# Differential attention: the first two weight units of the output projection are prepared piece by piece between the heads

## The chip, the cores and the metric

The kernel runs as one program on one core of a Trainium2 chip. The core has a matmul engine (PE, with its weight loads shown apart as PEld), a vector engine (DVE), a scalar engine (ACT), a general engine (POOL) and a queue engine (SP) that issues most of the transfers. Each engine works through its own instructions strictly in the order in which they were queued, and semaphores tie the engines together. The metric is the device time of one execution in microseconds; the time of a kernel is the median of several runs.

## The reference

One inference step of a two-layer decoder. Layer 0 is gated linear attention, layer 1 differential attention; a squared-ReLU MLP and a layer norm follow each. There are 1024 new prompt tokens behind 16 meta tokens, and eight running sequences with a paged cache of 4096 keys. The change touches layer 1's prompt attention and the projection behind it. Cut to what matters:

```python
q, k, v = diff_project(x, w_in, pos)                 # 8 heads, each with two 64-wide q/k halves
s = einsum('bqhmd,bkhmd->bhmqk', q, k) * 64 ** -0.5  # two score maps per head
p = softmax(where(k_pos <= q_pos, s, -inf))
o = einsum('bhqk,bkhe->bqhe', p[:, :, 0] - lam * p[:, :, 1], v)
out = (rms_norm(o, g_sub) * (1 - lam_init)) @ w_out  # w_out is 1024 x 1024
x = layer_norm(ALPHA * x + out)
```

## The kernel before

All matrix products are taken in a split form: an fp32 operand is cast to a shorter type (`hi`) and the rest (`lo` = operand - `hi`) is kept beside it, and three matmuls make one product. A weight matrix is therefore handled in *units* of 1024 rows by 256 columns. `unit` (L182 to L196) makes one from four *pieces*. A piece is a transfer of 256 KB into a tile `raw` (L191, issued by SP), a cast into `whi` on ACT (L193) and a subtraction into `wlo` on POOL (L194). The pool of `raw` has two buffers, those of `whi` and `wlo` have two each, so two units can be held, and the transfer of a piece must wait until the subtraction two pieces earlier is done. `kunit` (L198) calls `unit` on a slice of columns.

Prompt attention is a list of 64 steps: 8 heads times 8 tiles of 128 query rows. In heads 0 to 6 the tiles come in the order 7, 1, 5, 3, 6, 0, 4, 2, counted by n = 0 to 7; tile t looks at 16 + 128(t+1) keys. A step has two halves:

- `front` (L1348): the two score maps on PE in blocks of up to 512 keys (L1366), masking and row minimum on DVE (L1368), two exponentials with row sums on ACT (L1370), the reciprocal and the combination of the two maps on DVE (L1372 to L1374). The last of these, L1374, is appended to `joined`; its width tells the tile (1040 is n = 0, 656 is n = 6).
- `back` (L1378): transposes of the combined map on PE (L1387), in groups of up to four key blocks, each copied to SBUF by ACT (L1389, appended to `copied`), and the product with the values on PE (L1392). Tile 7 has groups of 512, 512 and 128 columns; tile 6 has 512 and 512; tile 5 has 512 and 384.

Every fourth step ACT moves the result out (L1493) and takes four sums of squares (L1497). Score maps have five buffers (`scp`). Between the steps lie the preparation of the next head's keys and queries (`prep`, with a cast on ACT and a subtraction on DVE, L202 and L203), the loads of the next heads by SP (`load_qk` L1224, `load_v` L1337), the scaling of finished heads on DVE (`scale_piece`, L1410, in pieces of 128x512, two at the end of heads 2, 4 and 6 and two at the start of heads 3 and 5; its power is taken on POOL, L1403) and, at the end of head 3 and in head 4, the projection of the eight samples (`samples_rows`, weight rows `sw` loaded at L1439 by SP, products at L1449 on PE).

The text of the program is not the order on an engine. A planner walks through it with a cost model, gives each instruction a priority by its place in the text, and appends it to its engine's queue when the model says that it is ready and nothing of higher priority is. `tc.issue_after(ins)` adds one tie: instructions written in its block that run on the engine of `ins` are queued behind `ins`. Transfers, which SP issues, and subtractions on POOL get no such tie when `ins` is on ACT.

`w_out` (L1045) multiplies by the output weights, in the order of (unit, half of the tokens) (0,0), (1,0), (0,1), (1,1), (2,0), (3,0), (2,1), (3,1), and takes a unit in when its number comes up first. It is written behind the attention, and its first products run beside head 7. For unit 0 it uses the tie (L1051):

```python
with tc.issue_after(out_after) if scaled and u == 0 else nullcontext():
    units[u] = kunit(w, u * 256)
```

where `out_after` is the latest transposed copy that the text has reached at head 2, n = 3 (L1480), which is the last copy of tile 5 of that head.

Of the kernel before, what the change touches and what calls it, by code (L numbers as in the profile page):

```python
# [11 lines left out]
F32 = mybir.dt.float32  # L12
F32R = mybir.dt.float32r
# [3 lines left out]
ALU = mybir.AluOpType  # L17
# [4 lines left out]
P = 128  # L22
# [92 lines left out]
def hybrid_step(ctx, tc, A, dbg=None, upto=9):  # L115
    nc = tc.nc
    V, S, G, TE = nc.vector, nc.scalar, nc.gpsimd, nc.tensor
    dma = nc.sync.dma_start
# [5 lines left out]
    wsp = ctx.enter_context(tc.tile_pool(name="wsp", bufs=2))  # L124
    wrp = ctx.enter_context(tc.tile_pool(name="wrp", bufs=2))
# [56 lines left out]
    def unit(n, *srcs):  # L182

        hi = wsp.tile([P, 2048], F32R, name="whi")
        lo = wsp.tile([P, 2048], F32R, name="wlo")
        at = 0
        for src in srcs:
            step = 512 // n
            for x in range(0, src.shape[1], step):
                raw = wrp.tile([P, 512], F32, name="raw")  # L190
                dma(raw.rearrange("p (k n) -> p k n", n=n), src[:, x : x + step, :])  # L191
                c = slice(at, at + 512)
                S.copy(hi[:, c], raw)  # L193
                G.tensor_tensor(lo[:, c], raw, hi[:, c].bitcast(F32), op=ALU.subtract)  # L194
                at += 512
        return hi, lo  # L196

    def kunit(w, c0):  # L198
        return unit(256, w.rearrange("(k p) n -> p k n", p=P)[:, :, c0 : c0 + 256])
# [322 lines left out]
    first = proj(0)  # L522
# [10 lines left out]
    for k in range(NB):  # L533
        w = sload(wi[k * P : (k + 1) * P, 0:2048])
# [6 lines left out]
    for k in range(0, NB, 2):  # L541
        w = sload2(wi[:, 2048:3072], k)
# [56 lines left out]
    for hh in range(2):  # L599
        ps = smt()  # L600
        for i in range(2):
            h = 2 * hh + i
# [16 lines left out]
    for s in (8, 4, 2, 1):  # L619
        u = t2()[:, :128]  # L620
# [231 lines left out]
    for h in range(GH):  # L852
        hi, lo = kunit(wi, 2048 + h * 256)
# [188 lines left out]

    def w_out(w, scaled, side=None):  # L1045

        units = {}
        n = 0
        for u, c in ((0, 0), (1, 0), (0, 1), (1, 1), (2, 0), (3, 0), (2, 1), (3, 1)):
            if u not in units:  # L1050
                with tc.issue_after(out_after) if scaled and u == 0 else nullcontext():  # L1051
                    units[u] = kunit(w, u * 256)
            hv, lv = (x.rearrange("p (k n) -> p k n", n=256) for x in units[u])
            for i2 in range(2):
                ps = mmt()
                t0 = 4 * c + 2 * i2
                for i in range(2):
                    a = slice((t0 + i) * P, (t0 + i + 1) * P)
                    for k in range(NB):
                        mm3(ps[:, i * 256 : (i + 1) * 256], XH[:, k, a], XL[:, k, a], hv[:, k, :], lv[:, k, :], k == 0, k == NB - 1)  # L1060
                yv = Yt[:, t0 : t0 + 2, u * 256 : (u + 1) * 256]
                pv = ps.rearrange("p (i n) -> p i n", n=256)
                if scaled:
                    steps_v.append(V.tensor_tensor(yv, yv, pv, op=ALU.add).ins)
                else:
                    steps_v.append(V.scalar_tensor_tensor(yv, yv, ALPHA, pv, ALU.mult, ALU.add).ins)
                if side and (n == 4 if scaled else n < 12):
                    next(side)
                n += 1
                if u % 2:  # L1070
                    for t in (t0, t0 + 1):
                        yield t, u // 2
# [9 lines left out]
    def normalize(steps, stats, done, last=None, behind=None):  # L1082

        st, mv, rs = stats
        half = set()
        for t, j in steps:
            if last and t not in (2, 3):
                if t in half:
                    last(t, mv, rs)
                half.add(t)  # L1090
                continue
            V.bn_stats(st[:, t, j, :], Yt[:, t, j * 512 : (j + 1) * 512])  # L1092
            if t not in half:
                half.add(t)
                continue
            V.bn_aggr(mv[:, t, :], st[:, t])  # L1096
            if t % 2 == 0 and not last:
                continue
            ts = slice(t if last else t - 1, t + 1)
            V.tensor_scalar(rs[:, 0, ts], mv[:, ts, 1], EPS, None, ALU.add)  # L1100
            steps_g.append(G.tensor_tensor(rs[:, 0, ts], rs[:, 0, ts], mhalf[:, : ts.stop - ts.start], op=ALU.pow).ins)
            if last:
                last(t, mv, rs)
                continue
            if behind is not None and t % 4 == 1:
                held = ts
                continue
            for ts in (held, ts) if behind is not None else (ts,):
                with tc.issue_after(behind[-1]) if behind is not None else nullcontext():
                    V.scalar_tensor_tensor(rs[:, 1, ts], mv[:, ts, 0], -1.0, rs[:, 0, ts], ALU.mult, ALU.mult)  # L1110
                for x in range(ts.start, ts.stop):
                    S.activation(Yt[:, x, :], Yt[:, x, :], AF.Identity, bias=rs[:, 1, x : x + 1], scale=rs[:, 0, x : x + 1])
            if t % 4 == 3:
                done(t // 4)

    def to_fm(c, ln, dst=None):
        cs = slice(512 * c, 512 * c + 512)
        for k in range(NB):
            ps = axt()
            for i in range(4):  # L1120
                TE.transpose(ps[:, i * P : (i + 1) * P], Yt[:, 4 * c + i, k * P : (k + 1) * P], ident)
            out = ps if dst is None else dst(c)[:, k, :512]
            g, b = lnp[:, ln, 0, k : k + 1], lnp[:, ln, 1, k : k + 1]
            if k % 2:
                i = V.tensor_scalar(out, ps, g, b, ALU.mult, ALU.add).ins
            else:
                S.activation(out, ps, AF.Identity, bias=b, scale=g)
            if dst is None:
                i = split(XH[:, k, cs], XL[:, k, cs], ps).ins
            steps_v.append(i)  # L1130
# [212 lines left out]
        dma(vx, vr[NM:].rearrange("(t p) d -> p t d", p=P))  # L1343
        return vm, vx

    joined, copied, pend = [], [], []

    def front(h, t, ks, qs):  # L1348
        W = NM + P * (t + 1)
# [111 lines left out]
    for step in steps + [None] * 0:  # L1461
        if step:
            h, n, t = step
            if h < 7:
                if n == 0:
                    nxt = prep(h + 1, *raws[h + 1])
                for _ in range(((1, 1, 2, 0) if h else (0, 1, 1, 2))[n] if n < 4 else 0):
                    heads[h + 1] = next(nxt)
                if n == 3:
                    vals[h + 1] = load_v(h + 1)  # L1470
                elif n == 5 and h < 6:
                    raws.append(load_qk(h + 2))
            if h == 3 and n == 7 or h == 4 and n < 4:
                next(srows)
            todo.append((step, front(h, t, *heads[h])))
            if pend and (h == 7 or (8 * h + n - 6) % 16 < 4):
                with tc.issue_after(joined[-1]):
                    scale_piece()
            if (h, n) == (2, 3):
                out_after = copied[-1]  # L1480
            if (h, n) == (0, 0):
                late(3)
                values_tile()
        if step and len(todo) <= 0:
            continue
        (h, n, t), sc_ = todo.pop(0)
        if n % 4 == 0:
            po = smt()
        at = t % 4 if h == 7 else t // 2
        back(t, sc_, po[:, at * P : (at + 1) * P], *vals[h])  # L1490
        if n % 4 == 3:
            ts = (slice(0, 4), slice(4, 8))[n // 4] if h == 7 else slice(t % 2, 8, 2)
            S.copy(Yd[:, ts, h], po.rearrange("p (t e) -> p t e", e=P))  # L1493
            for i in range(4):
                x = po[:, i * P : (i + 1) * P]
                j = ts.start + i * (ts.step or 1)
                S.activation(x, x, AF.Square, accum_out=oss[:, j, h : h + 1])  # L1497
        if n == 3 and h == 7:
            XH.t[0][1] = xh_part(0, 1)
            o_norm(slice(0, 4), slice(7, 8))  # L1500
            while pend:
                scale_piece()
            for j in range(8):
                o_fm(j, 0)
        elif n == 7 and h < 6 and h % 2:
            o_norm(slice(0, 8), slice(h - 1, h + 1))
        elif n == 7 and h == 6:
            o_norm(slice(0, 8), slice(6, 7))
# [60 lines left out]
    def samples():  # L1569

        sev = s2()
        dma(sev, A["srow"])
        s_post(sev, 2, hp)
        yield

    stats = ln_stats(hp)
    normalize(w_out(A["diff_w_out"][0], True, samples()), stats, lambda c: to_fm(c, 2, xr), None, steps_v)
    if upto == 4:
        dbg(locals())
        return e.close()  # L1580
# [276 lines left out]
```

## Time and profile before

| | |
|---|---|
| time, median of 3 runs | 2794.14 us (2793.73 to 2798.08) |
| the profiled execution's own time | 2787.8 us |
| its span, first to last instruction | 2785.6 us |
| mean granted clock of PE | 0.996 |
| busy share PE / DVE / ACT / POOL | 98% / 69% / 41% / 39% |
| attention heads, 1742 to 2004 us of the span | PE 239.88 of 262 us |
| behind them to the second MLP, 2004 to 2075 us | PE 71.00 of 71 us |

Rows of the view in order of time give the start in us from the span's start, the length in us, engine, line, operation, output<-inputs, shapes, and a count where equal neighbours are merged; in brackets stands the idle time of the engine before the instruction, and what ended it. Rows of the view of windows give the stretch, its length, and for each engine the busy time and the number of instructions, then the granted clock of PE, the busy share of the DMA engines and GB/s.

### The profile page before, as it was taken

Reading aid. Unit: us, or ns where it says so; the run is one execution under the profiler, and the core shown is the slowest. Engines: PE = TensorE matmul, PEld = TensorE weight load, DVE = VectorE, ACT = ScalarE, POOL = GpSimd, SP = SyncE. Lnnn points to the kernel's source line nnn. Section 1 sums busy time; section 2 is a strip of 40 time slices with the busy share of each in tenths; the row PEclk is TensorE's granted clock in tenths of the full one; section 3 lists DMA queues with packets and bytes.
Section 4 is the critical chain, followed back from the end, with each engine's and each line's share of the span. In section 5 each row is a group of like instructions: output and inputs, shape, how many; then the busy total and the mean of one; then the engine's idle time right before and its main releaser. Section 6 shows DMA issues by size and latency. Waiting matters only on the chain. (4 is left out here: it accounts for less than half of the span.)

```text
span 2785.6 us, 52274 instructions
## 1 busy us (share of the span) xinstructions
PE 2716.1 (98%) x19849; PEld 2230.6 (80%) x19849; DVE 1908.2 (69%) x3000; ACT 1130.0 (41%) x2316; POOL 1089.4 (39%) x736
## 2 busy tenths in 40 slices
PE   8999999999999999999999999999999999999998
PEld 5867767987777777777799988776899889798986
DVE  5365453678877777777667740787747888978687
ACT  4344463152221221221242112677625646355554
POOL 2112212234344343334323321120025767786775
PEclk9999999999999999999999999999999999999999
DMA  7575645735898898988748995122143554664585
GB/s 237 167 244 192 222 155 185 263 96 186 292 329 317 310 351 297 345 306 314 264 146 319 353 374 182 54 77 80 39 126 73 122 140 103 136 138 106 131 188 119
DMA packets 276392, 562.81 MB, mean 202 GB/s; under 512 B 23510, under 2 KB 144412, under 8 KB 272044
## 3 DMA queue, kind: packets, MB, share of 16 engines
q1 hardware_dynamic: 256076, 522.75, 54.1%
q0 software_dynamic: 20064, 36.71, 8.1%
q8 instruction: 156, 2.56, 0.4%
q14 instruction: 96, 0.79, 0.1%
HBM read 533.00 MB, written 29.52 MB: 202 GB/s over the span
## 5 line engine op out<-in xcount | busy, mean ns | idle before, releaser
L194 POOL TENSOR_TENSOR wlo<-raw,whi 128x512 fp32r<-128x512 f32 x252 | 366.1, 1467 | 715.0 <-ACT whi L193 571.6
L206 PE MATMUL mmt<-whi,XH 128*128 128x256 f32 (+1 forms) x1744 | 519.1, 300 | 1.1 <-DVE ast L1368 0.9
L207 PE MATMUL mmt<-wlo,XH 128*128 128x256 f32 (+1 forms) x1744 | 516.5, 297 | 0.4 <-POOL wlo L194 0.4
L206 PE MATMUL mmt<-XH,whi 128*128 128x512 f32 (+1 forms) x1216 | 434.5, 359 | 4.0 <-DVE HL L203 1.9
L208 PE MATMUL mmt<-XH,wlo 128*128 128x512 f32 (+1 forms) x1216 | 432.1, 356 | 0.2 <-POOL wlo L1681 0.2
L208 PE MATMUL mmt<-whi,XL 128*128 128x256 f32 x1520 | 427.1, 284 | 0.0
L193 ACT CAST whi<-raw 128x512 fp32r<-128x512 f32 x252 | 150.6, 621 | 567.0 <-PE mmt L208 190.2
L206 PEld LDWEIGHTS mmt<-whi,XH 128*128 128x128 f32 x1744 | 326.9, 188 | 38.9 <-issue 23.5
L953 DVE TENSOR_REDUCE sc<-pg 128x16 f32<-128x1024 f32 x256 | 308.6, 1212 | 71.1 <-POOL pg L952 68.6
L207 PEld LDWEIGHTS mmt<-wlo,XH 128*128 128x128 f32 x1744 | 328.3, 188 | 17.4 <-issue 7.2
L207 PE MATMUL mmt<-XL,whi 128*128 128x512 f32 x768 | 307.3, 401 | 0.0
L952 DVE TENSOR_TENSOR pg<-pg,qb 128x1024 f32<-128x1024 f32 x192 | 262.6, 1375 | 62.2 <-DMA pg<-in_cache_k 55.7
L208 PEld LDWEIGHTS mmt<-whi,XL 128*128 128x128 f32 x1520 | 284.5, 188 | 5.5 <-issue 5.0
L206 PEld LDWEIGHTS mmt<-XH,whi 128*128 128x128 f32 x1216 | 229.0, 189 | 51.0 <-issue 10.8
L952 POOL TENSOR_TENSOR pg<-pg,qb 128x1024 f32<-128x1024 f32 x64 | 166.2, 2599 | 258.9 <-DMA pg<-in_cache_k 157.7
L208 PEld LDWEIGHTS mmt<-XH,wlo 128*128 128x128 f32 x1216 | 229.5, 189 | 34.9 <-issue 2.5
L206 PE MATMUL mmt<-whi,HH 128*128 128x512 f32 x512 | 204.7, 401 | 4.6 <-DVE Y L1186 3.1
L208 PE MATMUL mmt<-whi,HL 128*128 128x512 f32 x512 | 203.9, 398 | 0.0
L207 PE MATMUL mmt<-wlo,HH 128*128 128x512 f32 x512 | 203.4, 397 | 0.0
L1681 POOL TENSOR_TENSOR wlo<-rw,whi 128x512 fp32r<-128x512 f32 x92 | 156.2, 1759 | 87.9 <-ACT whi L1680 87.9
L1681 POOL TENSOR_TENSOR wlo<-RW,whi 128x512 fp32r<-128x512 f32 x96 | 165.6, 1752 | 58.0 <-ACT whi L1680 58.0
L207 PEld LDWEIGHTS mmt<-XL,whi 128*128 128x128 f32 x768 | 145.3, 189 | 38.7 <-issue 7.2
(453 smaller groups left out, 5695.0 us busy)
## 6 DMA issues: line engine op xcount, KB each, us to landing
pg<-in_cache_k SPq DMA_DIRECT2D x256, 512.0 KB
pg<-in_cache_v SPq DMA_DIRECT2D x256, 512.0 KB
raw<-in_mlp_w SPq DMA_DIRECT2D x164, 256.0 KB
swt<-in_mlp_w SPq DMA_DIRECT2D x32, 1024.0 KB
rw<-in_mlp_w SPq DMA_DIRECT2D x116, 256.0 KB
RW<-in_mlp_w POOLq DMA_DIRECT2D x96, 256.0 KB, 5.7
swt<-in_gla_w_in SPq DMA_DIRECT2D x12, 1024.0 KB
swt<-in_diff_w_in SPq DMA_DIRECT2D x12, 1024.0 KB
```

The lines of the kernel that those rows point to most:

```text
L193: S.copy(hi[:, c], raw)
L194: G.tensor_tensor(lo[:, c], raw, hi[:, c].bitcast(F32), op=ALU.subtract)
L206: TE.matmul(ps, ah, bh, start=first, stop=False)
L207: TE.matmul(ps, ah, bl, start=False, stop=False)
L208: return TE.matmul(ps, al, bh, start=False, stop=last)
L952: eng.tensor_tensor(pg, pg, qb, op=ALU.mult)
L953: return V.tensor_reduce(sc[:, n, :], pg.rearrange("p (h d) -> p h d", d=64), op=ALU.add, axis=AX.X).ins
L1681: G.tensor_tensor(lo[:, k, :], t, hi[:, k, :].bitcast(F32), op=ALU.subtract)
```

## The change

A generator `unit_pieces` does the same work as `unit` on the same tiles and returns after each piece. The loop of attention calls it in heads 2 to 5 at n = 1 and n = 5: the four pieces of unit 0 in heads 2 and 3, those of unit 1 in heads 4 and 5. Each cast is tied behind the latest transposed copy that the text has reached at that point, which is the last copy of the step before (tile 7 for n = 1, tile 6 for n = 5). `w_out` gets the finished units as an argument; its own tie goes away, and units 2 and 3 are made in it as before.

```diff
+    def unit_pieces(w, c0):
+        hi = wsp.tile([P, 2048], F32R, name="whi")
+        lo = wsp.tile([P, 2048], F32R, name="wlo")
+        src = w.rearrange("(k p) n -> p k n", p=P)[:, :, c0 : c0 + 256]
+        yield hi, lo
+        for at in range(0, 2048, 512):
+            raw = wrp.tile([P, 512], F32, name="raw")
+            dma(raw.rearrange("p (k n) -> p k n", n=256), src[:, at // 256 : at // 256 + 2, :])
+            c = slice(at, at + 512)
+            S.copy(hi[:, c], raw)
+            G.tensor_tensor(lo[:, c], raw, hi[:, c].bitcast(F32), op=ALU.subtract)
+            yield
...
-    def w_out(w, scaled, side=None):
+    def w_out(w, scaled, side=None, units={}):
-        units = {}
+        units = dict(units)
...
             if u not in units:
-                with tc.issue_after(out_after) if scaled and u == 0 else nullcontext():
-                    units[u] = kunit(w, u * 256)
+                units[u] = kunit(w, u * 256)
...
-            if (h, n) == (2, 3):
-                out_after = copied[-1]
+            if 2 <= h < 6 and n in (1, 5):
+                u = h // 4
+                if u not in first:
+                    pieces = unit_pieces(A["diff_w_out"][0], u * 256)
+                    first[u] = next(pieces)
+                with tc.issue_after(copied[-1]):
+                    next(pieces)
...
-    normalize(w_out(A["diff_w_out"][0], True, samples()), stats, ...)
+    normalize(w_out(A["diff_w_out"][0], True, samples(), first), stats, ...)
```

More of the change, by code (lines that the diff above doesn't have):

```diff
@@ L1344, in load_v @@
         return vm, vx
-    joined, copied, pend = [], [], []
+    joined, copied, pend, first = [], [], [], {}
     def front(h, t, ks, qs):
@@ L1576, in hybrid_step @@
     stats = ln_stats(hp)
-    normalize(w_out(A["diff_w_out"][0], True, samples()), stats, lambda c: to_fm(c, 2, xr), None, steps_v)
+    normalize(w_out(A["diff_w_out"][0], True, samples(), first), stats, lambda c: to_fm(c, 2, xr), None, steps_v)
     if upto == 4:
```

## The prediction

> **What bounds the kernel now.** I read the page first: it says whether one engine sets the time.
>
> ```profile
> span 2785.6 us, 52274 instructions
> ...
> PE 2716.1 (98%) x19849; PEld 2230.6 (80%) x19849; DVE 1908.2 (69%) x3000; ACT 1130.0 (41%) x2316; POOL 1089.4 (39%) x736
> ```
>
> PE is busy 98% of the span, and where it idles is what a change can win. The view of windows, asked for the attention heads and for the stretch behind them, shows where that is.
>
> ```profile
> 1742.00:2004.00 262.00, 239.88 (x1883) 189.88 (x1882) 209.26 (x709) 195.68 (x545) 31.57 (x14) 0.98 0.21 62
> 2004.00:2075.00 71.00, 71.00 (x612) 71.00 (x611) 26.93 (x50) 18.27 (x38) 15.36 (x13) 1.00 0.48 139
> ```
>
> In the heads PE idles 262 - 239.88 = 22.1 us while DVE works 80% and ACT 75% of the time: the three pass work round, and a delay on one can reach PE. Behind them PE has no gap, so a time won in the heads is carried to the end.
>
> Next I measured the heads one by one, by the last DVE operation of a step's front (L1374) in the order of time: width 1040 is a head's n = 0, 656 its n = 6.
>
> ```profile
> 1781.09 1.30 DVE L1374 SCALAR_TENSOR_TENSOR as<-as,ast 128x1040 f32<-128x1040 f32 x1
> 1800.59 0.90 DVE L1374 SCALAR_TENSOR_TENSOR as<-as,ast 128x656 f32<-128x656 f32 x1
> ...
> 1811.78 1.30 DVE L1374 SCALAR_TENSOR_TENSOR as<-as,ast 128x1040 f32<-128x1040 f32 x1
> 1831.13 0.90 DVE L1374 SCALAR_TENSOR_TENSOR as<-as,ast 128x656 f32<-128x656 f32 x1
> ...
> 1844.26 1.30 DVE L1374 SCALAR_TENSOR_TENSOR as<-as,ast 128x1040 f32<-128x1040 f32 x1
> 1867.86 0.90 DVE L1374 SCALAR_TENSOR_TENSOR as<-as,ast 128x656 f32<-128x656 f32 x1
> ...
> 1879.05 1.30 DVE L1374 SCALAR_TENSOR_TENSOR as<-as,ast 128x1040 f32<-128x1040 f32 x1
> ...
> 1918.85 1.30 DVE L1374 SCALAR_TENSOR_TENSOR as<-as,ast 128x1040 f32<-128x1040 f32 x1
> 1936.91 0.90 DVE L1374 SCALAR_TENSOR_TENSOR as<-as,ast 128x656 f32<-128x656 f32 x1
> ```
>
> Head 1 takes 1800.59 - 1781.09 = 19.50 us from n = 0 to n = 6 and 11.19 from there to the next head. Head 2 takes 19.35 and then 13.13; head 3 takes 23.60 and then 11.19; head 5 takes 18.06 for its first part. So the end of head 2 and the start of head 3 are long, and that is where ACT casts the two units:
>
> ```profile
> 1832.24 0.48 ACT L1389 COPY aT<-axt 128x384 f32<-128x384 f32 x1 [0.64 <-PE axt L1387]
> 1832.62 1.15 ACT L193 CAST whi<-raw 128x512 fp32r<-128x512 f32 x2
> ...
> 1843.85 0.62 ACT L193 CAST whi<-raw 128x512 fp32r<-128x512 f32 x1 [0.95 <-DMA raw<-in_diff_w_out]
> ...
> 1849.39 0.62 ACT L193 CAST whi<-raw 128x512 fp32r<-128x512 f32 x1 [1.27 <-DMA raw<-in_diff_w_out]
> ...
> 1851.86 0.62 ACT L193 CAST whi<-raw 128x512 fp32r<-128x512 f32 x1
> 1852.38 0.58 ACT L1493 COPY Y<-smt 128x512 f32<-128x512 f32 x1
> ```
>
> All eight casts lie in 1832.6 to 1852.4, not four: unit 1 follows unit 0 at once. A cast holds ACT for 1852.38 - 1851.86 = 0.52 us, and a cast whose piece has not landed holds back all that is queued behind it. From the waits, over heads 2 and 3:
>
> ```profile
> ACT whi L193 <- DMA raw<-in_diff_w_out: 3.0, 3, 1.3
> ```
>
> (total, times, longest.) PE pays for it in two long gaps and, by the window of head 3, in its clock:
>
> ```profile
> 1845.28 0.49 PE L1392 MATMUL smt<-vm,aT 128*128 128x128 f32 x2 [1.83 <-ACT aT L1389]
> 1856.09 0.34 PE L1366 MATMUL prt<-XH 64*128 64x144 f32 x2 [2.19 <-DVE ast L1368]
> 1844.26:1879.05 34.79, 31.52 (x233) 25.47 (x233) 28.84 (x96) 27.24 (x76) 6.75 (x4) 0.90 0.26 77
> ```
>
> The first gap ends with a copy queued behind the cast of 1843.85, the second with DVE work whose exponentials were queued behind the cast of 1849.39. A clock of 0.90 over 34.79 us is 3.5 us of PE time lost.
>
> **The change part by part.** *Removed: the burst.* The end of head 2 is 13.13 - 11.19 = 1.94 us longer than that of head 1, the start of head 3 23.60 - 19.50 = 4.10 longer than head 1's. Together 6.04 us; with head 5's start as the measure (like head 3's it has two scaling pieces) it is 1.94 + 5.54 = 7.48. Head 5 comes behind head 4, which PE's sample products stretch, so it may start ahead; I take 6.04. The burst's own work, 8 x 0.52 + 3.0 = 7.2 us of ACT, is of this size.
>
> Of this, the clock could be a part apart. *By the Trainium skill ("TensorE: Matmul & The Clock Gate", Part 1) the clock halves only after an idle window of about 3.4 us. The trace has no gap as long as that, and yet the clock falls in the window with the gaps of 1.83 and 2.19. By the rule these gaps would not be the cause, and 3.5 of the 6.04 us would stay.* By the row they are, and I count them as removed.
>
> *Added: eight casts at other places.* Put on the old time axis, the casts land behind the last copies of tiles 7 and 6 of heads 2 to 5. Each piece then has some 15 us and its transfer is long done, so the waits of 3.0 us go; each still holds ACT 0.52. Together between 0 and 8 x 0.52 = 4.16 us. What lies there is seen in heads 5 and 4:
>
> ```profile
> 1928.42 0.26 ACT L1389 COPY aT<-axt 128x128 f32<-128x128 f32 x1
> ...
> 1943.35 0.61 ACT L1389 COPY aT<-axt 128x512 f32<-128x512 f32 x1
> ...
> 1905.02 0.59 ACT L1389 COPY aT<-axt 128x512 f32<-128x512 f32 x1 [3.35 <-PE axt L1387]
> ...
> 1932.55 0.49 PE L1392 MATMUL smt<-vm,aT 128*128 128x128 f32 x2 [0.27 <-ACT aT L1389]
> ...
> 1948.42 0.49 PE L1392 MATMUL smt<-vm,aT 128*128 128x128 f32 x2 [0.53 <-ACT aT L1389]
> ```
>
> Behind the cast of n = 5 (after 1943.35) are queued the sums of squares and the exponentials of the next head's first tiles, then the copy for which PE waits 0.53 us: full price, in heads 2, 3 and 5. Behind that of n = 1 (after 1928.42) PE waits 0.27 for ACT once; I charge one of the three such casts in full. In head 4 ACT itself waits 3.35 us for PE, and two casts hide there. Four of eight: 2.08 us. Without head 4's cover it would be 1.04 more.
>
> *Moved: eight subtractions on POOL.* In the burst one scaling piece and one tiny operation of DVE overlap them:
>
> ```profile
> 1844.55 3.82 POOL L194 TENSOR_TENSOR wlo<-raw,whi 128x512 fp32r<-128x512 f32 x2 [3.41 <-ACT whi L193]
> ...
> 1845.47 1.76 DVE L1410 TENSOR_TENSOR Y<-Y,orr 128x512 f32<-128x512 f32 x1
> 1849.24 0.22 DVE L1373 SCALAR_TENSOR_TENSOR ast<-ast,lamv,ls 128x1 f32<-128x1 f32 x1
> 1849.91 0.68 DVE L1410 TENSOR_TENSOR Y<-Y,orr 128x512 f32<-128x512 f32 x1
> 1852.55 1.28 POOL L194 TENSOR_TENSOR wlo<-raw,whi 128x512 fp32r<-128x512 f32 x1 [0.81 <-ACT whi L193]
> ...
> 1852.89 0.96 DVE L1373 SCALAR_TENSOR_TENSOR ast<-ast,lamv,ls 128x1 f32<-128x1 f32 x1
> ```
>
> They take 1.76 for 0.68 and 0.96 for 0.22: 1.08 + 0.74 = 1.82 us for eight subtractions. Spread, each can meet DVE again: from 0 to 8 x 1.28 = 10.2 us; nearest is the row of the same operation, 1.82, of which half on the path makes 0.9. *The Trainium skill ("SBUF — State Buffer", Who interferes with whom) says that DVE and POOL share a pair of ports under an exclusive lock. These rows agree. By that alone each subtraction could cost its 1.28, which is the slower rival below.*
>
> *Moved: eight transfers on SP.* The first two are issued early in either kernel, the others follow the subtractions.
>
> ```profile
> 1706.39 3.80 SPq L191 DMA_DIRECT2D raw<-in_diff_w_out  x2
> ...
> 1834.62 14.14 SPq L191 DMA_DIRECT2D raw<-in_diff_w_out  x6
> ...
> 1891.23 5.74 SPq L1439 DMA_DIRECT2D sw<-in_diff_w_out  x3
> ```
>
> The third to sixth pass the loads of heads 4 to 6, which are needed a head later. The seventh falls at about 1896, among the rows `sw`: queued ahead of one, it could hold it for as long as the fifth subtraction is late. Bounds: 0, and the 1.28 of a subtraction; I take 0. The ninth and tenth, for unit 2, go out at about 1940 instead of in that row of six and two more, and unit 2 is used behind 2004: nothing.
>
> Sum: -6.04 + 2.08 + 0.9 = -3.06 us. The profiled execution would go from 2787.8 to 2784.7. It lies 6.3 us below the median of the runs; on the median, 2794.14 - 3.06 = 2791.1.
>
> **The rivals.** *B, all pieces hide and the heads run like head 5:* 7.48 us won, 2786.7. For it: ACT waits for PE in each head, five score maps buffer the steps. Against: the 0.53 gap stands already without a cast. Chance 0.26.
>
> *C, the clock falls anyway:* the removed part is 6.04 - 3.5, and the sum 2.54 - 2.98 = -0.4 won, 2794.6. For it: the rule above. Against: the window of head 3 with its two gaps. Chance 0.13.
>
> *D, slower: each subtraction stops DVE in the heads.* Before, most fell into DVE's idle time in the burst, when DVE waited for ACT; spread out, they meet a DVE that is 80% busy. At 8 x 1.28 = 10.2 and 2.08 for the casts the sum is 6.3 us slower, 2800.4. It decides once a subtraction costs more than (6.04 - 2.08) / 8 = 0.50 us. Against: 1.82 / 8 = 0.23 before. Chance 0.14.
>
> *E, the change doesn't do what it says:* the tie holds a cast only from one side, and the planner may queue pieces late and close together. Two neighbours then pay a wait of about 1 us each (0.95 and 1.27 above) again, in two or three places: 2 us of the gain go, 2793. Chance 0.07.
>
> **How the numbers follow.** The forecast (A) has 0.40, with its own range 2788 to 2794 (casts wholly hidden, or 4.16 and 1.82 paid). About 0.2% or 5.6 us is what a measurement here can tell. Faster by more than that: B and the edge of A, 0.31. Slower: D, 0.14. The rest, 0.55, is no change. The range leaves out D and a tip of B: 2785 to 2798.5.
>
> **What would show it.** Casts with no wait for `raw` in the heads, eight places some 12 to 20 us apart; head 2's end at about 11.5 us and head 3's start at about 20; a clock of 1.00 there; no PE gap over 1.2 us in heads 2 to 5; heads 4 and 5 longer by at most 1 us. The prediction is wrong if the heads before and after sum to the same (C), if L1368 or L1374 grow beside L194 (D), or if PE's gap at the ends of heads 2 to 5 passes 1.5 us and the clock falls there.

## The result and the profile after

The changed kernel takes 2783.91 us against 2794.1 us before (medians of 16 runs each): a ratio of 0.9964, with a 95% interval of 0.9954 to 0.9975, or 7.0 to 12.9 us faster. The forecast of 2791.1 us was 7 us too high, the measured time lies 1.1 us below the range, and what was given the most weight, no change, is not what came.

The page of the changed kernel:

```profile
span 2780.6 us, 52281 instructions
...
PE 2710.2 (97%) x19849; PEld 2228.5 (80%) x19849; DVE 1922.7 (69%) x3000; ACT 1125.0 (40%) x2316; POOL 1083.5 (39%) x736
```

The five engines run as many instructions as before, and PE is busy 6 us less. The span is only 5.0 us shorter than that of the first trace, which is half of what the runs show; the last section says where the other half went. The heads tell it cleanly. Here are the same marks as in the prediction, in the order of time (the line has moved from L1374 to L1386):

```profile
1810.29 1.30 DVE L1386 SCALAR_TENSOR_TENSOR as<-as,ast 128x1040 f32<-128x1040 f32 x1
1829.65 0.90 DVE L1386 SCALAR_TENSOR_TENSOR as<-as,ast 128x656 f32<-128x656 f32 x1
...
1841.92 1.30 DVE L1386 SCALAR_TENSOR_TENSOR as<-as,ast 128x1040 f32<-128x1040 f32 x1
1859.90 0.90 DVE L1386 SCALAR_TENSOR_TENSOR as<-as,ast 128x656 f32<-128x656 f32 x1
...
1870.79 1.30 DVE L1386 SCALAR_TENSOR_TENSOR as<-as,ast 128x1040 f32<-128x1040 f32 x1
1893.61 0.90 DVE L1386 SCALAR_TENSOR_TENSOR as<-as,ast 128x656 f32<-128x656 f32 x1
...
1905.45 1.30 DVE L1386 SCALAR_TENSOR_TENSOR as<-as,ast 128x1040 f32<-128x1040 f32 x1
```

| from n = 0 to the next head's n = 0, us | before | after | |
|---|---|---|---|
| head 2 | 32.48 | 31.63 | -0.85 |
| head 3 | 34.79 | 28.87 | -5.92 |
| head 4 | 39.80 | 34.66 | -5.14 |
| head 5 | 29.24 | 30.33 | +1.09 |
| head 6 | 28.26 | 29.01 | +0.75 |

Together -10.07 us, close to the 10.2 us between the medians. Heads 0, 1 and 7 agree within 0.03. Head 3 was forecast; head 4 was not.

These marks sit at the end of a step's *front*. The fronts run ahead of the backs: up to five score maps are in flight. The copy that takes four finished steps out (L1493 before, L1510 after) marks the other end. First and last mark of heads 2 and 3, and the end of head 4, before and then after:

```profile
1819.35 0.59 ACT L1493 COPY Y<-smt 128x512 f32<-128x512 f32 x1 [1.71 <-PE smt L1392]
...
1889.28 0.57 ACT L1493 COPY Y<-smt 128x512 f32<-128x512 f32 x1
...
1923.48 0.59 ACT L1493 COPY Y<-smt 128x512 f32<-128x512 f32 x1
```

```profile
1817.84 0.59 ACT L1510 COPY Y<-smt 128x512 f32<-128x512 f32 x1 [1.72 <-PE smt L1404]
...
1878.89 0.57 ACT L1510 COPY Y<-smt 128x512 f32<-128x512 f32 x1
...
1911.10 0.58 ACT L1510 COPY Y<-smt 128x512 f32<-128x512 f32 x1
```

By finished work heads 2 and 3 take 69.93 us before and 61.05 after (-8.88), and head 4 takes 34.20 and 32.21 (-1.99). So of the 5.14 us that the front marks give to head 4, some 3 are a loss of heads 2 and 3 that shows there late.

The casts stand apart now. The rows show the first two and the last in the order of time, and the view of tiles has only one entry in which ACT waits for the output weights, that of units 2 and 3 (L193; the pieces are L207):

```profile
1822.81 0.64 ACT L207 CAST whi<-raw 128x512 fp32r<-128x512 f32 x1
...
1836.43 0.62 ACT L207 CAST whi<-raw 128x512 fp32r<-128x512 f32 x1
...
1931.81 0.64 ACT L207 CAST whi<-raw 128x512 fp32r<-128x512 f32 x1
  ACT whi L193: 13.6, 5
```

None of the eight waits for its transfer. None of PE's gaps in heads 2 to 6 is longer than 0.79 us, and the window of head 3 shows the full clock (it was 0.90):

```profile
1841.92:1870.79 28.87, 27.07 (x227) 22.30 (x227) 24.83 (x87) 23.44 (x66) 2.57 (x2) 1.00 0.26 73
```

### The profile page after: what moved, and what is told of

Same layout as the page of the kernel before. It is cut to its first block, busy times and chain, and to the rows that moved or that the text cites. A ratio compares the mean times of both kernels' runs of the same rounds, so it can differ in the third digit from the quotient of the medians.

```text
span 2780.6 us, 52281 instructions
## 1 busy us (share of the span) xinstructions
PE 2710.2 (97%) x19849; PEld 2228.5 (80%) x19849; DVE 1922.7 (69%) x3000; ACT 1125.0 (40%) x2316; POOL 1083.5 (39%) x736
## 5 line engine op out<-in xcount | busy, mean ns | idle before, releaser
L194 POOL TENSOR_TENSOR wlo<-raw,whi 128x512 fp32r<-128x512 f32 x244 | 352.7, 1460 | 704.4 <-ACT whi L193 628.3
L193 ACT CAST whi<-raw 128x512 fp32r<-128x512 f32 x244 | 145.3, 619 | 556.1 <-PE mmt L221 185.8
```

## The experiments

The measure for all of them is the time of heads 2 to 7, from head 2's n = 0 to the last mark of head 7, which repeated within 0.3 us in two traces of one kernel (188.32 and 188.38; 178.67 and 178.44), while the times of whole runs lie up to 19 us apart. For the two kernels the last marks are these, so that the measure is 2000.10 - 1811.78 = 188.32 us before and 1988.55 - 1810.29 = 178.26 after:

```profile
2000.10 0.90 DVE L1374 SCALAR_TENSOR_TENSOR as<-as,ast 128x656 f32<-128x656 f32 x1
```

```profile
1988.55 0.90 DVE L1386 SCALAR_TENSOR_TENSOR as<-as,ast 128x656 f32<-128x656 f32 x1
```

| kernel | heads 2 to 7, us |
|---|---|
| before; before, again | 188.32; 188.38 |
| changed | 178.26 |
| no pieces at all | 179.06 |
| subtraction twice; cast twice | 179.98; 185.27 |
| piece at every second step (two runs); at every step | 178.67, 178.44; 181.92 |
| unit 0 in a burst, unit 1 apart | 179.95 |
| burst without waits, same place | 184.82 |
| burst in heads 5 and 6 | 182.79 |
| before with samples later; changed with samples later | 186.41; 179.76 |
| before with scaling later | 188.04 |
| changed with paired rows; before with paired rows | 178.24; 187.20 |

Where the time lies on PE can be read from windows over the whole measure, here of the kernel before, the changed kernel and the one with no pieces. Each holds 1357 matmuls:

```profile
1811.78:2000.10 188.32, 173.81 (x1357) 136.12 (x1354) 150.35 (x505) 144.98 (x412) 22.24 (x13) 0.98 0.22 64
```

```profile
1810.29:1988.55 178.26, 166.78 (x1357) 133.11 (x1354) 150.42 (x506) 143.04 (x412) 20.63 (x13) 1.00 0.22 68
```

```profile
1815.04:1994.10 179.06, 168.17 (x1357) 133.01 (x1354) 148.49 (x505) 140.13 (x404) 10.41 (x5) 1.00 0.18 56
```

Idle is the length less PE's busy time. The part lost to the clock is half of the time at half clock; the products of the samples have a view of their own.

| kernel, us of heads 2 to 7 | in all | PE idle | lost to the clock | sample products | other products |
|---|---|---|---|---|---|
| before | 188.32 | 14.51 | 3.41 | 8.42 | 161.98 |
| changed | 178.26 | 11.48 | 0 | 6.34 | 160.44 |
| no pieces at all | 179.06 | 10.89 | 0 | 7.38 | 160.79 |
| cast twice | 185.27 | 16.55 | 0 | 7.29 | 161.43 |
| piece at every step | 181.92 | 13.88 | 0 | 7.38 | 160.66 |
| burst without waits | 184.82 | 14.93 | 1.71 | 7.38 | 160.80 |
| changed with paired rows | 178.24 | 13.06 | 0 | 4.26 | 160.92 |

**What do the spread pieces still cost?** All three steps of the pieces are left out (in the edit the reshaping of the two old units isn't shown).

```diff
-            if 2 <= h < 6 and n in (1, 5):
+            if False:
...
-    normalize(w_out(..., samples(), first), ...)
+    normalize(w_out(..., samples(), {0: units[10], 1: units[11]}), ...)
```

> The changed kernel without the eight pieces: w_out's units 0 and 1 are not fetched, cast or split at all, and its products read the last two units of the projection before instead, which still lie in the buffers. Measured over heads 2 to 6 (from head 2's n = 0 to head 7's n = 0, by L1374 before and L1386 after), the kernel before takes 1976.35 - 1811.78 = 164.57 us and the changed kernel 1964.79 - 1810.29 = 154.50. Theory 1 (the spread pieces are nearly hidden, as the trace after suggests in heads 2 and 3): 153 to 154.5. Rival, the price of the prediction (2.08 for the casts and 0.9 for the subtractions): 151.5. In time: ratio to before 0.995 to 0.997 either way. If head 4's gain of 5.15 us comes from the absence of the burst ahead of it, head 4 stays near 34.7 us here.

```profile
1815.04 1.30 DVE L1386 SCALAR_TENSOR_TENSOR as<-as,ast 128x1040 f32<-128x1040 f32 x1
...
1994.10 0.90 DVE L1386 SCALAR_TENSOR_TENSOR as<-as,ast 128x656 f32<-128x656 f32 x1
```

179.06 us, 0.8 more than with the pieces. The ratio to the kernel before is 0.9978 (0.9965 to 0.9991), whose interval overlaps that of the changed kernel. Heads 2 to 6 take 154.90, just above the first theory's 153 to 154.5 and far from the 151.5 of the prediction's price; head 4 takes 34.45, so its gain does come from the absence of the burst. By the table PE idles 0.6 us less without the pieces, and its sample products take 1.04 us more because they stand in seven groups instead of six. That order of PE's queue was not planned, and the changed kernel is lucky in it. The spread pieces cost nothing that can be told from this order, and 2.08 + 0.9 us of the forecast fall.

**Each piece's parts doubled.** The subtraction on POOL twice, and, in another kernel, the cast on ACT twice.

```diff
             G.tensor_tensor(lo[:, c], raw, hi[:, c].bitcast(F32), op=ALU.subtract)
+            G.tensor_tensor(lo[:, c], raw, hi[:, c].bitcast(F32), op=ALU.subtract)
```

> The changed kernel with the subtraction on POOL done twice in each of the eight pieces. Theory 1 (a subtraction on POOL rarely meets DVE): heads 2 to 6 take 154.5 to 155.5 us, under 0.13 us each. Rival D of the prediction (each can hold DVE for its 1.28 us): 154.5 + 8 x 0.6 to 8 x 1.28 = 159 to 165.

The measure is 179.98: 1.72 us for eight more subtractions, 0.22 each. Heads 2 to 6 take 156.23, between the two theories' figures. The slower rival's 1.28 each is out. How much of the 1.72 is the order of PE's queue, which moved the kernel without pieces by 0.8, isn't separated.

```diff
             S.copy(hi[:, c], raw)
+            S.copy(hi[:, c], raw)
```

> The changed kernel with the cast on ACT done twice in each of the eight pieces, so 16 casts in heads 2 to 5. Heads 2 to 7 took 178.26 us with one cast each and 179.06 with none. Theory B (casts that are ready and apart are absorbed by ACT's own waits for PE): 178 to 180. Rival, the price of the prediction (four of eight casts cost their 0.52 us): 178.26 + 2.1 = 180.4 or more.

```profile
1819.34 1.30 DVE L1387 SCALAR_TENSOR_TENSOR as<-as,ast 128x1040 f32<-128x1040 f32 x1
...
2004.61 0.90 DVE L1387 SCALAR_TENSOR_TENSOR as<-as,ast 128x656 f32<-128x656 f32 x1
```

185.27 us, 7.0 more: the first theory is out, and the rival's "180.4 or more" holds, but at three times the price that it named. The eight added casts hold ACT 8 x 0.52 = 4.2 us and cost 0.88 each. The planner put each second cast 0.8 to 3.1 us behind the first, behind other work of the step, and turned PE's queue elsewhere. Of the 7.0 us, 5.1 are idle PE and 1.9 longer products; the two causes aren't separated here. So a second cast at these places wasn't free.

**How far apart must the pieces be?** Every second step in heads 2 and 3, every step from head 2, n = 3, and a burst of unit 0 alone:

```diff
-            if 2 <= h < 6 and n in (1, 5):
-                u = h // 4
+            if 2 <= h < 4 and n % 2:
+                u = h - 2
```

> The changed kernel with its pieces at every second step of heads 2 and 3 (n = 1, 3, 5, 7; unit 0 in head 2, unit 1 in head 3) instead of every fourth of heads 2 to 5. Heads 2 to 7 took 178.26 us with every fourth step, 181.92 with every step, 188.32 before. Theory B (a cast is free as long as ACT has caught up before the next one): 178 to 180. Rival (each cast costs a part of its 0.52 us and the place decides): between the two, 180 to 181.

> The changed kernel with a piece behind every second step of heads 2 and 3, timed. Its heads 2 to 7 took 178.67 us against 178.26, so the time should be that of the changed kernel: ratio to before 0.9955 to 0.9975. The other view, that its single time of 2774.99 us was more than chance: under 0.995.

```diff
-            if 2 <= h < 6 and n in (1, 5):
-                u = h // 4
+            if 19 <= 8 * h + n < 27:
+                u = (8 * h + n - 19) // 4
```

> The changed kernel with its eight pieces behind eight steps in a row, from head 2, n = 3 to head 3, n = 2, instead of every fourth step. Each piece's transfer can start only when the subtraction two pieces earlier is done. Theory 1 (the price of a burst is the casts' waits for transfers, which fall on ACT's queue): several casts wait for raw, together 2 to 4 us, and heads 2 and 3 take 63 to 66 us against 60.49. Rival (the price is in the casts and their order, at one per step already absorbed): 60.5 to 62 with waits of under 1 us.

```diff
-            if 2 <= h < 6 and n in (1, 5):
+            if (h, n) == (2, 3):
+                with tc.issue_after(copied[-1]):
+                    first[0] = kunit(A["diff_w_out"][0], 0)
+            if 4 <= h < 6 and n in (1, 5):
```

> The changed kernel with unit 0 made at once behind head 2, n = 3 (four casts in a row, as before) and unit 1 piece by piece in heads 4 and 5 only. Theory 1 (the price of a burst is its waits for transfers: unit 0's first two pieces are landed long ago, only two casts can wait): heads 2 and 3 lie 1 to 3 us over the changed kernel's 31.63 + 28.86 = 60.49, head 4 stays at about 34.7. Rival (the price is the eight casts of 0.52 us and the clock's fall, which two PE gaps of about 2 us bring): four casts cost half of the burst, 3 to 3.5 us, with a fall of the clock in head 3.

Every second step is as good as every fourth: 178.67 and 178.44, and timed a ratio of 0.9968 (0.9954 to 0.9981). Its first single time of 2775 us is at the low end of the twelve runs timed later (2774.89 to 2790.05). At every step the heads take 181.92, with no cast waiting for its transfer and no gap of PE over 1.2 us: 2.9 us over the kernel without pieces, from eight casts that hold ACT 4.2. By the table these 2.9 us are idle PE (13.88 against 10.89) and nothing else. Heads 2 and 3 take 63.33, as the first theory had it, without its waits: the cost came, the waits did not. Four casts at once and four apart take 179.95, within 0.9 of no casts. Heads 2 and 3 grow by 0.6 us there (61.12 against 60.49), less than either theory said, though one cast waits 0.75 us.

**A burst without waits.** All eight casts stand behind head 2, n = 3, but work on two landed tiles; the other six transfers are left out.

```diff
-            if 2 <= h < 6 and n in (1, 5):
...
+            if (h, n) == (2, 3):
+                for u in range(2):
+                    pieces = unit_pieces(A["diff_w_out"][0], u * 256)
+                    first[u] = next(pieces)
+                    with tc.issue_after(copied[-1]):
+                        list(pieces)
...
-            raw = wrp.tile([P, 512], F32, name="raw")
-            dma(raw.rearrange("p (k n) -> p k n", n=256), src[:, at // 256 : at // 256 + 2, :])
+            if len(raws2) < 2:
+                raws2.append(wrp.tile([P, 512], F32, name="raw"))
...
+            raw = raws2[at // 512 % 2]
```

> The changed kernel with all eight pieces at once behind head 2, n = 3, but only the first two transfers are made: the other six casts and subtractions read the same two tiles again (six transfers are left out, so the units hold the wrong numbers). No cast can wait for a transfer; the planner queues all eight in a row, 8 x 0.52 = 4.2 us of ACT. Heads 2 to 7 (to the last L1386) take 188.32 us before, 178.26 in the changed kernel and 179.06 without casts. Theory W (the burst's price is the waits for transfers and what the clock does after them): 179 to 182. Theory B (the price is ACT being kept from the copies and exponentials, whatever keeps it): a block of 4.2 us makes a PE gap of over 1.8 us and a fall of the clock, 183 to 186.

The first two rows are the measure's ends, then the casts on ACT, PE's longest gap and the window behind it:

```profile
1818.98 1.30 DVE L1391 SCALAR_TENSOR_TENSOR as<-as,ast 128x1040 f32<-128x1040 f32 x1
...
2003.80 0.90 DVE L1391 SCALAR_TENSOR_TENSOR as<-as,ast 128x656 f32<-128x656 f32 x1
...
1839.78 4.26 ACT L212 CAST whi<-raw 128x512 fp32r<-128x512 f32 x8
...
1850.84 0.44 PE L1383 MATMUL prt<-XH 64*128 64x384 f32 x2 [3.06 <-DVE ast L1385]
1852.20:1855.60 3.40, 3.40 (x18) 3.40 (x17) 3.07 (x11) 1.07 (x6) 0.00 (x0) 0.50 0.25 77
```

184.82 us: 5.8 over no pieces, with no wait for a transfer at all. Theory B held: it is enough that ACT is kept from the copies and exponentials by work alone. ACT is held 4.26 us on end here; PE's gap opens 3.7 us after the last cast (1850.84 - 3.06, against 1839.78 + 4.26), and behind it PE runs at half clock. By the table the 5.8 us are 4.04 of idle PE, nearly as long as ACT was held, and 1.71 lost to the clock. In the kernel before ACT was held 8 x 0.52 + 3.0 = 7.2 us, over 20 us, and that cost 188.32 - 179.06 = 9.3: 3.6 of idle PE, 3.4 of clock, 1.0 in the sample products and 1.2 in the others.

**The same burst elsewhere.** Only the tie of the kernel before is moved.

```diff
-            if (h, n) == (2, 3):
+            if (h, n) == (5, 3):
                 out_after = copied[-1]
```

> The kernel before with its tie moved from head 2, n = 3 to head 5, n = 3: the same burst of eight casts, three heads later. Theory 1 (the burst costs what it costs wherever it stands, because its casts wait for their transfers, and head 4 is slow before only because the burst went ahead of it and turned the order of PE's queue): heads 2 to 4 take about what they take in the changed kernel (31.6, 28.9, 34.7), and heads 5 and 6 together about 6 to 7 us more than its 30.33 + 29.02; time to before about 0.998. Rival (the burst hurts only beside the sample products of heads 3 and 4): heads 5 and 6 grow by less than 3 us, time at 0.996 to 0.997.

Ends of the measure, PE's longest gap and the window behind it:

```profile
1813.25 1.30 DVE L1374 SCALAR_TENSOR_TENSOR as<-as,ast 128x1040 f32<-128x1040 f32 x1
...
1996.04 0.90 DVE L1374 SCALAR_TENSOR_TENSOR as<-as,ast 128x656 f32<-128x656 f32 x1
...
1944.08 0.48 PE L1366 MATMUL prt<-XH 64*128 64x464 f32 x2 [1.63 <-DVE ast L1368]
1945.54:1948.95 3.41, 3.41 (x16) 2.49 (x15) 2.91 (x11) 2.84 (x9) 1.57 (x2) 0.50 0.25 77
```

182.79 us: here the burst costs 3.7 us, not 9.3, though its casts wait as long (3.2 us). Heads 2 to 4 take 31.59, 29.07 and 34.72, as in the changed kernel. Heads 5 and 6 take 3.9 us more than there. The theory that it costs the same wherever it stands (6 to 7) falls, and the rival (under 3) isn't met either; the timed ratio is 0.9987 (0.9972 to 1.0002), which includes no change. In heads 2 to 6 it has 2.05 us more idle PE than the kernel without pieces, 1.71 lost to the clock, and nothing else. One fall of the clock there instead of two is 1.7 us of the difference (half of 3.41).

**Is it the sample products of head 4?** Both kernels with these products two heads later.

```diff
-            if h == 3 and n == 7 or h == 4 and n < 4:
+            if h == 5 and n == 7 or h == 6 and n < 4:
                 next(srows)
```

> The kernel before with the sample products moved from the end of head 3 and head 4 to the end of head 5 and head 6; the burst stays. Theory 1 (head 4's 5 us came from sample products that the burst put into a worse place of PE's queue): heads 2 and 3 stay at 66 to 67.5 us, head 4 falls to 28.5 to 30 and head 6 rises to about 34.5; heads 2 to 6 take about 160. Rival (the burst leaves the pipeline behind, samples or not, and head 4 pays): head 4 takes 32 or more and heads 2 to 6 take 164 again.

> The changed kernel with the same move of the sample products. Theory 1: heads 2 to 6 take about 153.5 to 154.5 us, so that the change is worth 5.5 to 7 us there instead of 10. Rival: 154.5 against 164, a change worth 10 as before.

The ends of the measure, before and then changed:

```profile
1816.29 1.30 DVE L1374 SCALAR_TENSOR_TENSOR as<-as,ast 128x1040 f32<-128x1040 f32 x1
...
2002.70 0.90 DVE L1374 SCALAR_TENSOR_TENSOR as<-as,ast 128x656 f32<-128x656 f32 x1
```

```profile
1814.36 1.30 DVE L1386 SCALAR_TENSOR_TENSOR as<-as,ast 128x1040 f32<-128x1040 f32 x1
...
1994.12 0.90 DVE L1386 SCALAR_TENSOR_TENSOR as<-as,ast 128x656 f32<-128x656 f32 x1
```

186.41 and 179.76: without the products in head 4 the change is worth 6.65 us instead of 10.06. Head 4 falls only to 31.60 in the first, between the two expectations, and keeps 33.30 in the second. By finished work the burst still costs heads 2 and 3 8.3 us there (68.18 against 59.84), and head 4 makes 2.4 of them good (28.51 against 30.88); with the products in head 4 it loses 2.0 more instead. So some 3.4 us of the change's gain hang on the products' place, and the rest doesn't.

**Is it how the products are grouped?** In PE's queue before, the 32 products of the samples stand in eight groups, in the changed kernel in six. With both rows of a pair in one transfer they stand in four.

```diff
-            t = a1.tile([P, D], F32, name="sw%d" % (k % 2))
-            dma(t, wd_[k * P : (k + 1) * P, :])
-            return t
+            t = a1.tile([P, 2, D], F32, name="sw")
+            dma(t, wd_[k * P : (k + 2) * P, :].rearrange("(i p) n -> p i n", p=P))
+            return [t[:, 0], t[:, 1]]
```

> The changed kernel with the samples' weight rows fetched two at a time into one tile, so that the eight products of a pair of rows stand together in PE's queue (four groups of eight instead of two of eight and four of four). In the changed kernel a group of eight took 1.06 us and one of four 1.05. Theory G (a group costs 1.05 us whether it has four or eight): L1461's busy time falls from 6.34 to 4.2 us and heads 2 to 7 from 178.26 to about 176. Rival (the larger transfers come too late for the next pair): PE waits for sw by more than the 2.1 us that the groups save, 178 to 181. In time to the kernel before 0.995 to 0.997.

> The kernel before with the same pairing, burst unchanged: five groups (one of them split six and two) instead of eight. Theory G (2 of the 5 us of head 4 are groups of four, the rest idle PE): L1449's busy time falls from 8.42 to about 5.2 us, head 4 from 39.5 to 36 or 37, heads 2 to 7 from 188.35 to 184.5 to 186. Rival (head 4 is long because of the burst's aftermath): head 4 stays over 38.5.

Windows of 45 us with the products alone: before, changed, changed with paired rows.

```profile
1870.00:1915.00 45.00, 8.42 (x32) 1.15 (x32) 1.00 0.38 115
```

```profile
1860.00:1905.00 45.00, 6.34 (x32) 0.89 (x32) 1.00 0.46 146
```

```profile
1860.00:1905.00 45.00, 4.26 (x32) 0.63 (x32) 1.00 0.48 147
```

The busy time falls as theory G has it, 1.05 us a group. The heads don't follow: 178.24 against 178.26, because of the 2.08 us saved 1.58 come back as idle PE (13.06 against 11.48) and 0.48 in the other products; the ratio is 0.9968 (0.9954 to 0.9981). In the kernel before the products fall to 5.30 us and head 4 to 36.89 by the front marks (39.80 and 39.25 without pairing), both as theory G has it; the rival's 38.5 is out. But heads 2 to 7 lose only 1.1 us (187.20). PE waited 2.25 us for a row there, and the clock was at half for three stretches of 3.41 us instead of two, which is 1.7 us more. So grouping is a real cost on PE, and taking it away is no gain where PE then waits for others.

**Scaling pieces out of the burst, and the kernel before again.**

```diff
-            if pend and (h == 7 or (8 * h + n - 6) % 16 < 4):
+            if pend and (h == 7 or (8 * h + n - 12) % 16 < 4):
```

> The kernel before with the four scaling pieces (L1410) moved six steps later, so that those of heads 0 and 1 fall into head 3, n = 4 to 7, behind the burst, instead of the middle of it. Heads 2 to 7 took 188.32 us. Theory P (the subtractions of the burst hold DVE through the scaling pieces, which are the only operations of DVE there that both wait for the same ports and are long): 185.5 to 187, no L1410 over 1 us. Rival (the gaps of PE come from ACT alone): 187.5 to 188.5.

> The kernel before, once more, to see how well the times of the heads repeat. If the order of the queues alone sets them, heads 2 to 6 take 164.57 us within 0.3, with the clock falling twice in head 3; if they hang on when transfers happen to land, they differ by a microsecond or more, and the 10.07 us between the two first traces is partly chance.

188.04 us, which looks like no effect, but the edit did more than was meant: the two pieces at the end of head 6 slid into head 7, which takes 28.59 instead of 23.75, while heads 2 to 6 fall by 5.1, with one fall of the clock instead of two and no scaling piece over 0.69 us. It can't be read for theory P. The kernel before repeats at 188.38, with the loss spread a little otherwise (head 3 35.56, head 4 39.25).

## Why the prediction was wrong

*The place and the kind of the loss were right.* Eight casts in a row, casts queued ahead of their transfers, two long gaps of PE, and a clock that fell behind them: all of it went, and what the heads won (10.07 us in one pair of traces) arrives at the end (10.2 between the medians).

*The step that failed is the size of the removed part: 6.04 us forecast, 188.32 - 179.06 = 9.3 by the kernel without pieces.* I counted the burst's loss in heads 2 and 3 alone and put the length of head 4 down to the sample products. For heads 2 and 3 it came near by its own marks (6.77 us), in part by luck: 1.08 us less was won at the end of head 2 and 1.52 more at the start of head 3. But head 4, with the same products, falls from 39.80 us to 34.45 when the pieces are left out, while heads 5 to 7 take 2.7 more. With five score maps in flight a late back shows in a later front: by the front marks heads 2 and 3 won 6.77 us and head 4 5.14, by the finished work 8.88 and 1.99.

Finished work alone would not have put the forecast right. It needs a reference too, and head 1 was a poor one. By the mark below head 1 finishes in 1819.35 - 1787.22 = 32.13 us, so the finished work of heads 2 and 3 gives 69.93 - 2 x 32.13 = 5.7.

```profile
1787.22 0.57 ACT L1493 COPY Y<-smt 128x512 f32<-128x512 f32 x1
```

Without the burst heads 2 and 3 finish in 61.05, faster than twice head 1. The other reference, head 5, worked out and left at 7.48, was nearer: head 3's first part did become 17.98 us, where head 5 had shown 18.06. The end of head 2 became 12.27, not 11.19. It is 12.28 without any piece, so the burst isn't what makes it longer than head 1's; its two scaling pieces may be.

*The price of the casts, 2.08 us, was wrong: nothing that can be told from the order of PE's queue.* The kernel without pieces takes 179.06 us, with them 178.26. I took the 0.53 us that PE waited for a copy behind that place as a sign that a cast there is paid in full. It isn't. Where the 0.52 us are taken up was not isolated. One cast every second step is still free; at every step the eight cost 2.9, and two at every fourth step cost 7.0 more.

*The subtractions:* the heads don't show the 0.9 us charged, yet the hold on DVE is there, and it grew. Beside the eight subtractions four operations of DVE in the changed kernel take 3.3 us longer than others of their kind, against 1.82 in the burst. Two of them follow; others like them take 0.77 and 0.22 us:

```profile
1852.35 1.35 DVE L1386 SCALAR_TENSOR_TENSOR as<-as,ast 128x528 f32<-128x528 f32 x1
...
1886.11 1.13 DVE L1385 SCALAR_TENSOR_TENSOR ast<-ast,lamv,ls 128x1 f32<-128x1 f32 x1
```

So the sign of rival D appeared (L1374 of before, now L1386, grew beside a subtraction), and its cost did not: by the table PE idles at most 0.6 us more than without pieces, and doubled the subtractions cost 0.22 us each, under the 0.50 from which D decides. That also answers the rule of the Trainium skill that was weighed ("SBUF — State Buffer", Who interferes with whom): the lock's full price of 1.28 us a subtraction doesn't reach the path. Rival D is out.

*The clock:* the row was the better guide. Rival C, by which 3.5 us would stay, is out: head 3 runs at 1.00. But the length of one gap isn't what decides. In heads 2 to 6 of the other kernels the clock halved at gaps of 1.63 us (the late burst) to 3.06 (the burst without waits), while gaps of 1.74, 2.25 and 2.31 us passed without a fall of their own. In head 7 of the late burst it halved where no gap of PE was longer than 0.63. The falls of one trace stand whole multiples of 3.41 us apart (1846.09 and 1856.33 before: three times 3.41), so the falls keep a beat, and what counts may be the 3.41 us ahead of one. The rows are the first of the two falls in head 3 of the kernel before and the one in head 7 of the late burst, each with the 3.41 us ahead of it:

```profile
1842.68:1846.09 3.41, 1.58 (x14) 1.26 (x14) 3.12 (x8) 2.46 (x9) 1.54 (x1) 1.00 0.19 65
1846.09:1849.50 3.41, 3.41 (x18) 2.65 (x16) 3.24 (x12) 1.63 (x6) 2.28 (x2) 0.50 0.26 79
```

```profile
1989.91:1993.32 3.41, 2.18 (x14) 1.33 (x13) 3.41 (x12) 3.41 (x11) 0.00 (x0) 1.00 0.50 154
1993.32:1996.73 3.41, 3.41 (x17) 3.41 (x18) 3.38 (x9) 2.31 (x9) 0.77 (x1) 0.50 0.00 0
```

PE was busy for 0.46 and 0.64 of the 3.41 us ahead. In the attention heads of all 17 traces, cut on this beat, the clock went from full to half only behind a stretch with PE busy for at most 0.65 of it; each stretch under 0.52 was followed by a fall, and of those between 0.52 and 0.65 only some. The fall in head 7 costs nothing that shows: head 7 takes 24.15 us with it and 24.16 in the kernel without pieces, which has none. The Trainium skill ("TensorE: Matmul & The Clock Gate", Part 1) gives about 3.4 us as the idle window; the stretches at half clock do last 3.41 us here, but PE needn't be idle for all of the one before.

*The transfers* cost nothing, as charged: no piece waited, and PE waited 0.17 us for one sample row. *Rival E* is out: the casts stand 13.6 to 18.3 us apart.

*Rival B* came closest, at 2786.7. It was given 0.26 for "all pieces hide", which is what happened, on top of a loss that was larger than any row I had used.

*What stays open.* The same burst costs 9.3 us in heads 2 and 3, 6.65 there with the sample products elsewhere (against the changed kernel with the same move), and 3.7 in heads 5 and 6. In heads 2 to 6 the early burst costs 5.9 us more than the late one: 1.8 of idle PE, 1.7 of clock, 1.0 in the sample products and 1.4 in the other products. This says where the time lies and not why. The 1.4 us, the smaller idle time at the later place and the 0.88 us of a second cast have no experiment of their own, and each of these kernels also has PE's queue in another order.

## What to carry to other kernels

A burst of cheap work on an engine that others wait for can cost more than its length: ACT held for 7.2 us cost 9.3, of which 3.4 went through the clock of PE. The same work, spread to one piece every second step with its transfers landed, cost nothing that could be told from another order of PE's queue. Before pricing a piece at a place, look how long the engine has until the next piece, not whether somebody waits behind it once. In a pipeline that runs ahead, follow a loss until the later stages agree again, by finished work as well as by fronts; marks at the front put a part of it one stage late.

## What the runs showed beyond this

One execution's span can hide half of a small gain. Behind the heads both programs hold the same work, and yet the stretch from the last mark of the heads to the end took 785.5 us in the first trace of before, 792.1 in that of the changed kernel, and 783 to 795 in the others. That is where the other half of the 10 us went. In the changed kernel's trace one subtraction of DVE took 8.68 us, and PE stood still for 4.00 behind it; in the trace of before the same line, shape and place took 1.43:

```profile
2140.13 8.68 DVE L216 TENSOR_TENSOR XH<-RX,XH 128x1032 fp32r<-128x1032 f32 x1 [3.77 <-ACT XH L215]
...
2150.47 0.39 PE L219 MATMUL axt<-XH,whi 128*128 128x258 f32 x1 [4.00 <-DVE HF L1743]
```

```profile
2153.09 1.43 DVE L203 TENSOR_TENSOR XH<-RX,XH 128x1032 fp32r<-128x1032 f32 x1 [4.44 <-ACT XH L202]
```

POOL was subtracting and issuing transfers for the first 7.57 of those 8.68 us, until 2144.31 + 3.39 = 2147.70, and then stood still:

```profile
2144.31 3.39 POOL L1698 TENSOR_TENSOR wlo<-rw,whi 128x512 fp32r<-128x512 f32 x2
2149.43 0.88 POOL L1696 DMA_DIRECT2D rw<-in_mlp_w  x1 [1.73 <-DMA rw<-in_mlp_w]
```

The last 1.11 us are about what the same operation takes undisturbed (1.22 at 2150.66). This fits the lock named above, with DVE held over several POOL instructions on end; no run isolated it. The same subtraction took 8.6 to 8.8 us in six of the 17 traces, whose stretch behind the heads took 790 to 795 us, and 1.4 to 1.8 in the other eleven (783 to 793).

And on PE eight products of 128x32 by 512 took 1.06 us where four took 1.05: the busy time of the 32 products follows the number of groups (8.42, 6.34 and 4.26 us for eight, six and four), not the number of products. Standing next to each other isn't all of it: in the kernel with each cast twice, two groups of four came right behind each other in PE's queue and took 2.02 us together.
